# Two attention stages, convolutions and w_out rearranged: SSD and modulation beside the second attention, half of w_out beside the convolutions

## The chip, the cores and the metric

The kernel runs on one core of a Trainium2 chip. The metric is the device time of one execution in microseconds, inputs in DRAM at the start, output in DRAM at the end. Three runs of the kernel before gave 1917.51, 1924.35 and 1926.78 us; the median is 1924.35. Engines go by the names of the profile: PE (TensorE's matrix multiplies), PEld (its weight loads), DVE (VectorE), ACT (ScalarE), POOL (GpSimd) and SP (SyncE). POOL and SP do little but issue transfers here.

## The reference

Two layers act on 512 latent tokens and 256 context tokens of width 1024, in fp32. In each layer the normed tokens are projected and go through four head groups of width 256, whose outputs are concatenated and projected back; an MLP follows. The core of it:

```python
def token_mixers(h, hc, w_in, w_out, ...):
    proj, projc = h @ w_in, hc @ w_in
    ya, yac = ssd_branch(proj[..., :OFF_B], projc[..., :OFF_B], ...)
    yb = hyena_seq(proj[..., OFF_B:OFF_C], ...)
    yw = window_attention(apply_rope(qw, cos, sin), apply_rope(kw, cos, sin), vw, kwc, vwc, attn_sink)
    yd = dense_attention(apply_rope(rms_norm(qd, q_norm), cos, sin), ..., vd, kdc, vdc)
    y = jnp.concatenate([ya, yb, yw, yd], axis=-1) @ w_out
    if not need_ctx:
        return y, None
    ...
    return y, yc

def squared_relu_mlp(h, w1, w2):
    return jnp.square(jax.nn.relu(h @ w1)) @ w2
```

SSD is a chunked state space scan in two directions. Hyena multiplies spectra twice (two gated long convolutions), here done with matmuls against cosine and sine tables. The windowed attention ("c" in the kernel) and the dense one ("d") have 4 query heads and 2 key heads of 64. Around both halves of a layer stand norms with scale, shift and gate from a modulation vector, c @ w_mod. In the last layer the context outputs aren't needed.

## The kernel before

Every large product is made of three matmuls (`mm3`, lines 298 to 300): an operand is split into a rounded high part (`hi`, line 265 on ACT or 267 on DVE) and the difference (`lo`, line 270 on DVE), and high x high, high x low and low x high add up in PSUM. Tokens are in blocks of 128, six in layer 0 (four latent, two context) and four in layer 1. Weights arrive on SP's queue in units of 512 KB into raw tiles `r`, and are split into `w` with a priority of 4000 (`load_units`, 337).

The order of each engine comes from a scheduler that takes the instructions in program order, shifted by the priority they were written under; each engine then runs its list in order and waits where an instruction isn't ready. Where buffers of a pool come round, the next user waits for the last reader. `weave` (203) interleaves several generators, so many steps of each in turn.

After the setup and the hyena filters, `layer` (1379) does per layer:

- One stage with the pools `attR` and `ppA`: attention "d", the projection of "c", attention "c", then the projections of hyena and SSD. A block of attention goes from PE (`ps`, 1249 and 1250) to a maximum on DVE (1256), exp on ACT (1263), a scaling on DVE (1269), transposes on PE (1286), the split of the result into `pt` on ACT and DVE, and the product with V on PE (1294). The output is stored to the DRAM tensor `yy` (`y_d`) on POOL's queue (1299). The projections fill PE in between, since nothing of the attentions is needed by them.
- A stage with `ppB`, called mixing below: hyena for the latent tokens, hyena for the context (layer 0 only), SSD and the modulation vectors of the next sub-layers, woven. SSD reads its inputs back from DRAM (`xb`), hyena from `us`, its tables from `in_fwd` and `in_inv` (tiles `ht`, on POOL's queue) and its spectra `hf` on SP's queue.
- `ysplit`: the attention outputs are loaded from `yy` and split on DVE.
- `w_out` (1486) for pairs of token blocks: all four units of w_out, in the order 2, 3 (attention), 1, 0 (hyena, SSD), into PSUM `py`; `gated_norm` (1301) squares on ACT and scales on DVE (1311); `residual` and the pre-norm follow; then the MLP.

## Time and profile before

| | |
|---|---|
| median of three runs | 1924.35 us |
| the profiled execution | 1919.0 us, its span 1917.2 us |
| PE, DVE, ACT busy in the span | 1790.2, 1297.7, 836.8 us |
| layer 0: attentions and projections / mixing / w_out and norm | 151 to 405 / 405 to 543 / 543 to 620 us |
| layer 1: the same | 1210 to 1405 / 1405 to 1499 / 1499 to 1560 us |

The times of the stages are those between the first instructions of one stage's bound engine and the next. A busy share says how long an engine's instructions lay on it, not that they were fast: matmuls are pipelined, so what one matmul costs is the distance to the next one's start. The granted clock is the share of full speed that TensorE got in a stretch; full speed is 2.4 GHz, the other level is 1.2.

### The profile page before, as it was taken

Reading aid. Unit: us, or ns where it says so; the run is one execution under the profiler, and the core shown is the slowest. Engines: PE = TensorE matmul, PEld = TensorE weight load, DVE = VectorE, ACT = ScalarE, POOL = GpSimd, SP = SyncE. Lnnn points to the kernel's source line nnn. Section 1 sums busy time; section 2 is a strip of 40 time slices with the busy share of each in tenths; the row PEclk is TensorE's granted clock in tenths of the full one; section 3 lists DMA queues with packets and bytes.
Section 4 is the critical chain, followed back from the end, with each engine's and each line's share of the span. In section 5 each row is a group of like instructions: output and inputs, shape, how many; then the busy total and the mean of one; then the engine's idle time right before and its main releaser. Section 6 shows DMA issues by size and latency. Waiting matters only on the chain.

```text
span 1917.2 us, 27370 instructions
## 1 busy us (share of the span) xinstructions
PE 1790.2 (93%) x10170; PEld 1482.7 (77%) x10170; DVE 1297.7 (68%) x2897; ACT 836.8 (44%) x1804; POOL 91.5 (5%) x176
## 2 busy tenths in 40 slices
PE   6899999978879999999999998899978789999998
PEld 2688888845668888888888888888866688888886
DVE  4878888877756656676666658988878563444446
ACT  4844565536515532322222327556546263332322
POOL 0120001011000000000000000000010000000000
PEclk9999999989989999999999999999989899999999
DMA  8531121278833244333333415112183243233232
GB/s 291 187 111 53 39 74 58 69 260 272 290 107 132 93 135 136 121 107 114 121 121 121 142 47 176 45 48 89 45 273 120 74 157 113 91 99 99 88 102 85
DMA packets 137597, 235.16 MB, mean 123 GB/s; under 512 B 12466, under 2 KB 77395, under 8 KB 137464
## 3 DMA queue, kind: packets, MB, share of 16 engines
q1 hardware_dynamic: 122920, 186.12, 30.2%
q0 software_dynamic: 14544, 47.30, 7.1%
q8 instruction: 80, 1.31, 0.3%
q14 instruction: 53, 0.43, 0.1%
HBM read 206.74 MB, written 26.64 MB: 122 GB/s over the span
## 4 chain that ended last, share of the span: by engine, by line
PE 76%; DVE 9%; issue 6%; DMA 4%; ACT 4%; POOL 1%; SPq 0%; DVEq 0%; ACTq 0%; POOLq 0%
PE pg L298 19%; PE pg L299 18%; PE pg L300 18%; PE po L1294 3%; PE py L298 2%; PE py L299 2%; PE pm L1286 2%; PE py L300 2%; PE ps L1249 1%; PE ps L1250 1%; PE pm L1206 1%; PE psd L1052 1%; DMA spec<-fk 1%; POOL spec L725 1%; DMA r<-in_w_mod_dram 1%
## 5 line engine op out<-in xcount | busy, mean ns | idle before, releaser
L265 ACT ACTIVATE w<-r 128x1024 fp32r<-128x1024 f32 (+1 forms) x176 | 186.6, 1061 | 348.1 <-PE pg L300 325.1
L270 DVE TENSOR_TENSOR w<-r,w 128x1024 fp32r<-128x1024 f32 (+1 forms) x176 | 214.1, 1223 | 106.1 <-ACT w L265 105.2
L298 PE MATMUL pg<-xl,w 128*128 128x512 f32 (+1 forms) x704 | 269.5, 386 | 2.2 <-DVE ya L1311 0.9
L300 PE MATMUL pg<-xl,w 128*128 128x512 f32 (+1 forms) x704 | 269.7, 384 | 0.0
L299 PE MATMUL pg<-xl,w 128*128 128x512 f32 (+1 forms) x704 | 269.7, 384 | 0.0
L298 PE MATMUL pg<-w,H 128*128 128x512 f32 x640 | 250.1, 391 | 0.0
L299 PE MATMUL pg<-w,H 128*128 128x512 f32 x640 | 249.2, 390 | 0.0
L300 PE MATMUL pg<-w,H 128*128 128x512 f32 x640 | 249.0, 389 | 0.0
L476 DVE SCALAR_TENSOR_TENSOR x<-r,scT,x 128x512 f32<-128x512 f32 x168 | 119.1, 746 | 71.7 <-DMA r<-in_w_mod_dram 71.7
L298 PEld LDWEIGHTS pg<-xl,w 128*128 128x128 f32 x704 | 132.6, 190 | 27.7 <-issue 2.2
L300 PEld LDWEIGHTS pg<-xl,w 128*128 128x128 f32 x704 | 133.3, 189 | 22.9
L299 PEld LDWEIGHTS pg<-xl,w 128*128 128x128 f32 x704 | 133.3, 189 | 22.2 <-DVE xl L270 0.2
L298 PEld LDWEIGHTS pg<-w,H 128*128 128x128 f32 x640 | 120.1, 188 | 26.8 <-issue 1.7
L300 PEld LDWEIGHTS pg<-w,H 128*128 128x128 f32 x640 | 120.1, 188 | 25.0
L299 PEld LDWEIGHTS pg<-w,H 128*128 128x128 f32 x640 | 120.2, 188 | 24.4
L1520 ACT ACTIVATE t<-pg 128x512 f32<-128x512 f32 (+1 forms) x100 | 50.4, 506 | 198.0 <-PE pg L300 198.0
L1551 DVE TENSOR_TENSOR ya<-pg,ya 128x512 f32<-128x512 f32 x120 | 81.8, 687 | 69.0 <-PE pg L300 68.7
L1522 DVE TENSOR_TENSOR t<-t 128x512 f32<-128x512 f32 (+1 forms) x100 | 58.1, 582 | 83.7 <-ACT H L1521 83.6
L300 PE MATMUL pg<-xc,w 128*128 128x256 f32 (+1 forms) x368 | 104.4, 284 | 0.0
L298 PE MATMUL pg<-xc,w 128*128 128x256 f32 (+1 forms) x368 | 103.3, 284 | 1.1 <-ACT xc L265 1.1
L299 PE MATMUL pg<-xc,w 128*128 128x256 f32 (+1 forms) x368 | 104.1, 284 | 0.0
L298 PE MATMUL pg<-w,xl 128*128 128x256 f32 (+1 forms) x320 | 93.0, 292 | 5.4 <-ACT qk L1113 2.5
(357 smaller groups left out, 3866.1 us busy)
## 6 DMA issues: line engine op xcount, KB each, us to landing
r<-in_mlp_w_dram SPq DMA_DIRECT2D x128, 512.0 KB
r<-in_w_mod_dram SPq DMA_DIRECT2D x80, 512.0 KB
r<-in_w_in_dram SPq DMA_DIRECT2D x40, 512.0 KB
ht<-in_inv_dram POOLq DMA_DIRECT2D x20, 512.0 KB, 5.4
ht<-in_fwd_dram POOLq DMA_DIRECT2D x18, 512.0 KB, 5.4
wm<-in_w_mod_dram SPq DMA_DIRECT2D x16, 512.0 KB
r<-in_w_out_dram SPq DMA_DIRECT2D x16, 512.0 KB
xd<-x POOLq DMA_DIRECT2D x16, 512.0 KB, 3.3
```

The lines of the kernel that those rows point to most:

```text
L265: self.nc.scalar.activation(dst, src, AF.Copy)
L270: self.nc.vector.tensor_tensor(dst, src, h.bitcast(F32), SUB)
L298: mm(out, ah, bh, start=first, stop=False)
L299: mm(out, ah, bl, start=False, stop=False)
L300: mm(out, al, bh, start=False, stop=last)
L476: nc.vector.scalar_tensor_tensor(acc[:, c], raw[:, k], sc, acc[:, c], MUL, ADD)
L725: nc.gpsimd.dma_start(dst, kt[:, half, :])
L1286: nc.tensor.transpose(p[:, n:n + 128], P[:, col:col + 128], self.ident)
L1294: nc.tensor.matmul(po[:, qo:qo + m], V[:, c, :], pt[:, hl, cols[j]:cols[j] + m], start=i + j == 0 and hl == 0, stop=i + j == len(kts) - 1 ...
L1520: nc.scalar.activation(r, p[:, :nn], AF.Relu)
L1522: nc.vector.tensor_tensor(r, r, r, MUL)
L1551: nc.vector.tensor_tensor(dst, p, dst, ADD)
```

## The change

The projections of attention "c", SSD and hyena stand beside attention "d" alone, in that order (units z, x0, x1 before h0, h1, h2). Attention "c", SSD and modulation are woven in a stage of their own (`ppA2`), SSD in tiles that the projections and attention "d" used (`xl1`, `xc1`, `qk`, `V`). The attention's generator yields after each pair of blocks. `qk_split` transposes the raw q and k first and splits out of PSUM. Then come the convolutions, latent hyena with a priority of 4000 and context hyena with 1000, woven with `w_part`: the half of w_out that multiplies the attention outputs, per block of 128 tokens, evicted by ACT and stored on POOL's queue to a DRAM tensor `part`. `w_out` keeps units 1 and 0, and a DVE addition per block brings in `part`, which SP loads. `ysplit` is gone. Line numbers of the changed kernel differ: mm3 is at 299 to 301 there.

```diff
-        for br in "dc":
-            if br == "c":
-                self.qkv = self.qkv_in(l, br, XT)
-            qk, V = self.qkv
-            self.qk_prep(l, br, qk)
-            self.attention(l, br, qk, V)
+        self.do(self.attention(l, "d", *self.qkv))
+        self.qkv = self.qkv_in(l, "c", XT)
+        self.ssd_in(l, XT)
         self.hyena_in(l, XT)
-        self.ssd_in(l, XT)
+        self.pop(pp)
+
+        bk = {"ps": (1024, F32, 1), "po": (512, F32, 1), "pm": (512, F32, 3), "pd": (512, F32, 2)}
...
+        if mods:
+            bk.update({"pm": (512, F32, 2), "pmod": (512, F32, 1)})
+        pp = self.push("ppA2", bk, psum=True)
+        YT = self.new_xt((0,), need)
+        self.load_units(self.upos[l, "o", 3])
+        self.weave((self.attention(l, "c", *self.qkv), 1), (self.ssd(l, YT), 1), (chain(*mods), 3))
...
-        self.weave(*hys, (self.ssd(l, YT), W2[1]), (chain(*mods), W2[2]))
+        self.weave(*hys, (self.w_part(l, nt), 1))
...
+    def w_part(self, l, nt):
...
+        for t in range(nt):
+            y = self.t2((128, 4, 128))
+            nc.sync.dma_start(y, self.y_d[l][:, :, 128 * t:128 * t + 128].rearrange("c p t -> p c t"))
+            Y = [self.a("xl1", (4, 128)) for _ in range(2)]
+            self.hi(Y[0], y)
+            self.lo(Y[1], y, Y[0])
+            for q in range(2):
+                p = self.a("pw")
+                for c in (2, 3, 0, 1):
+                    w = self.utiles[l, "o", 2 + c // 2][q][:, :, c % 2]
+                    self.mm3(p, Y[0][:, c], Y[1][:, c], w[:, 0], w[:, 1], c == 2, c == 1)
+                o = self.t2()
+                nc.scalar.activation(o, p, AF.Copy)
+                nc.gpsimd.dma_start(self.part[l][t][:, 512 * q:512 * q + 512], o)
+                yield
...
-        order = (2, 3, 1, 0)
+        order = (1, 0)
...
+            nc.vector.tensor_tensor(ys[t], p, ys[t], ADD)
```

PE's list in layer 1, in the second attention. Before, between two blocks' `ps` rows and their transposes, stand rows of a projection (`pg`):

```order
L1249 MATMUL ps_13488<-QK_13262,QK_13260 128x256
L1250 MATMUL ps_13488<-QK_13263,QK_13260 128x256
L298 MATMUL pg_14205<-w_14119,xl_2105_11319 128x264
L299 MATMUL pg_14205<-w_14119,xl_2105_11319 128x264
L300 MATMUL pg_14205<-w_14119,xl_2121_11335 128x264
L298 MATMUL pg_14205<-w_14119,xl_2107_11321 128x264
L1286 MATMUL pm_13507<-ident,P_13481 128x128
L1286 MATMUL pm_13519<-ident,P_13481 128x128 x2
L1286 MATMUL pm_13530<-ident,P_13481 128x128
L299 MATMUL pg_14205<-w_14119,xl_2107_11321 128x264
```

The same place of the changed kernel (`pm` takes the attention's transposes, `po` its product with V):

```order
L1255 MATMUL ps_14062<-QK_13816,QK_13813 128x256
L1256 MATMUL ps_14062<-QK_13817,QK_13813 128x256
L1259 MATMUL ps_14062<-wmask,identr 128x256
L1255 MATMUL ps_14062<-QK_13816,QK_13813 128x256
L1256 MATMUL ps_14062<-QK_13817,QK_13813 128x256
L1292 MATMUL pm_14013<-ident,P_14006 128x128
L1292 MATMUL pm_14013<-ident,P_13987 128x128
L1292 MATMUL pm_14013<-ident,P_14006 128x128
L1292 MATMUL pm_14025<-ident,P_14006 128x128
L1292 MATMUL pm_14036<-ident,P_14006 128x128
L1300 MATMUL po_13891<-pt_14014,V_12717 128x256 x4
```

The projection rows have moved ahead of this place; here only the attention's own rows follow each other.

ACT's list in layer 1 at the start of the convolutions. `hx` are hyena's transformed inputs; ahead of them stood rows of SSD's convolution (`t`, line 735 and 914):

```order
L914 ACTIVATE t_14642<-t_14641 128x256
L734 ACTIVATE t_14680<-pg_14653 128x512
L735 ACTIVATE t_14678<-pg_14653,s_14409 128x512
L265 ACTIVATE hx_14739<-ph_2798_14734 128x512
L265 ACTIVATE hx_14773<-ph_2811_14768 128x512
```

In the changed kernel, where `xl_2801` is the high part of the first attention outputs, loaded back from `yy` into `t_14848`:

```order
L1305 ACTIVATE tA_14777<-po_14573 64x512
L266 ACTIVATE xl_2518_13757<-xl_2789_14808 128x512
L266 ACTIVATE xl_2519_13758<-xl_2791_14817 128x512
L266 ACTIVATE xl_2801_14850<-t_14848 128x512
L266 ACTIVATE hx_14845<-ph_2798_14840 128x512
L266 ACTIVATE hx_14875<-ph_2805_14870 128x512
```

The split of `w_part` stands ahead of both `hx` rows; before, nothing loaded from `yy` stood there. On DVE its low part stands ahead of the `hx` low parts too.

POOL's list in layer 1 at the same place. Before, the attention's last store stands three issues ahead of hyena's first tables, among stores of SSD's inputs:

```order
L1299 DMA yy_110<-yt_13684 128x512
L916 DMA xb_106<-t_14520 128x512
L916 DMA xb_106<-t_14557 128x256
L782 DMA ht_14793<-in_fwd_dram 128x1024
L916 DMA xb_106<-t_14604 128x512
L782 DMA ht_14833<-in_fwd_dram 128x1024
```

In the changed kernel:

```order
L1309 DMA yy_110<-yt_13890 128x512
L1309 DMA yy_110<-yt_14300 128x512
L784 DMA ht_14897<-in_fwd_dram 128x1024
L784 DMA ht_14945<-in_fwd_dram 128x1024
...
L1497 DMA part_0_117<-t_14867 128x512
L843 DMA ht_15316<-in_inv_dram 128x1024
L1497 DMA part_0_117<-t_14891 128x512
L843 DMA ht_15330<-in_inv_dram 128x1024
```

The tables now come directly after the last store of the attention, and the `part` stores come among and behind the later tables. On PE the last `pw` rows before `w_out`'s `py` in layer 1 read:

```order
L301 MATMUL pw_15126<-w_13685,xl_2852_15093 128x512
L299 MATMUL pw_15126<-w_13685,xl_2851_15092 128x512
L300 MATMUL pw_15126<-w_13685,xl_2851_15092 128x512
L301 MATMUL pw_15126<-w_13685,xl_2852_15093 128x512
L299 MATMUL py_15438<-wx_15417,xl_2520_13759 128x512
```

These rows stand behind the last hyena matmul; before, no such rows existed, and `py` followed on hyena.

## Rows read from the trace of the kernel before

**Rows 1.** Windows, layer 0: from:to, length, busy per engine, granted clock, DMA share, GB/s

```profile
151.00:405.00 254.00, 240.99 (x1618) 212.02 (x1617) 216.51 (x572) 144.15 (x372) 19.15 (x35) 0.98 0.22 69
190.00:300.00 110.00, 109.24 (x715) 94.86 (x716) 93.47 (x227) 67.34 (x168) 7.79 (x14) 1.00 0.18 55
405.00:543.00 138.00, 111.97 (x788) 74.72 (x788) 97.42 (x240) 67.99 (x207) 12.27 (x23) 0.87 0.78 261
426.00:543.00 117.00, 96.53 (x679) 66.69 (x679) 81.86 (x208) 61.80 (x192) 9.55 (x18) 0.88 0.75 253
400.00:426.00 26.00, 17.24 (x115) 9.13 (x115) 20.47 (x43) 7.39 (x17) 2.72 (x5) 0.75 0.94 312
543.00:620.00 77.00, 75.97 (x336) 62.01 (x337) 40.16 (x120) 31.43 (x55) 2.14 (x4) 0.96 0.40 141
```

**Rows 2.** Windows, layer 1

```profile
1210.00:1405.00 195.00, 185.89 (x1198) 158.95 (x1198) 166.69 (x413) 109.48 (x270) 10.44 (x19) 0.99 0.21 63
1405.00:1499.00 94.00, 65.48 (x394) 51.23 (x392) 73.75 (x166) 51.27 (x144) 9.61 (x18) 0.89 0.57 189
1405.00:1426.00 21.00, 9.93 (x45) 8.31 (x44) 12.62 (x21) 6.76 (x11) 4.84 (x9) 0.77 1.02 350
1470.00:1499.00 29.00, 17.27 (x122) 15.43 (x122) 25.60 (x62) 9.91 (x18) 1.06 (x2) 0.87 0.36 120
1499.00:1560.00 61.00, 56.80 (x256) 47.61 (x257) 33.87 (x87) 22.25 (x36) 2.14 (x4) 0.89 0.38 130
```

**Rows 3.** Chain of waits, layer 1, start of mixing: start us, us, what

```profile
1412.89 5.70 DMA xb<-t
1418.65 6.80 DMA sb<-xb
```

**Rows 4.** Chain of waits, layer 0, mixing

```profile
419.10 7.30 DMA ht<-in_inv_dram
...
485.86 5.57 DMA r<-in_w_mod_dram
...
496.70 5.29 DMA r<-in_w_mod_dram
```

**Rows 5.** Chain of waits, layer 1, w_out: an early and a later matmul

```profile
1501.17 0.43 PE py L299
...
1506.54 0.23 PE py L300
```

**Rows 6.** DVE groups, 151 to 405 us: line, shapes, count | busy, mean ns

```profile
L270 DVE TENSOR_TENSOR pt<-pm,pt 128x512 fp32r<-128x512 f32 x44 | 29.3, 688 | 8.8 <-ACT pt L265 8.4
...
L1256 DVE TENSOR_REDUCE s<-ps 128x1 f32<-128x768 f32 x16 | 15.3, 953 | 1.6 <-PE ps L1250 1.6
...
L270 DVE TENSOR_TENSOR sqk<-qk,sqk 128x128 fp32r<-128x128 f32 x48 | 12.2, 284 | 2.9 <-ACT sqk L265 2.9
...
L1209 DVE CAST QK<-pm 128x256 fp32r<-128x256 f32 x24 | 9.6, 419 | 0.6 <-ACT QK L1208 0.4
```

**Rows 7.** DMA issues: line, queue, count, KB each, median us to landing

```profile
us<-t POOLq DMA_DIRECT2D x12, 256.0 KB, 2.3
...
xb<-t POOLq DMA_DIRECT2D x8, 256.0 KB, 3.4
```

**Rows 8.** Chain of waits, layer 1, end of w_out, start of the MLP

```profile
1545.53 0.24 PE py L300
...
1552.48 0.58 PE pg L298
...
1559.13 0.48 PE pg L298 x4
```

**Rows 9.** Line L1311, the norm's last step: duration ns min/median/max

```profile
L1311 DVE SCALAR_TENSOR_TENSOR ya<-py,s,gt x10: 1273/1280/1284, 573.3 to 1551.2; 128x1024 f32<-128x1024 f32 x10
```

More of the change, by code (lines that the diff above doesn't have):

```diff
@@ L2 @@
 import math
-from contextlib import ExitStack
+from contextlib import ExitStack, nullcontext
 import numpy as np
@@ L203, in weave @@
     def weave(self, *gens):
-        live = [[g, n, self.st, self.lab] for g, n in gens]
+        live = [[g[0], g[1], self.st, self.lab, g[2] if len(g) > 2 else 0] for g in gens]
         while live:
@@ L209, in weave @@
                 self.mark(e[3])
-                for _ in range(e[1]):
-                    if next(e[0], self) is self:
-                        live.remove(e)
-                        break
+                with self.tc.high_priority(offset=e[4]) if e[4] else nullcontext():
+                    for _ in range(e[1]):
+                        if next(e[0], self) is self:
+                            live.remove(e)
+                            break
                 e[2], e[3] = self.st, self.lab
@@ L424, in setup @@
         self.y_d = [self.tc.dram_tile([4, 128, NTOK], F32, name=f"yy{l}") for l in range(self.nl)]
+        self.part = [[self.tc.dram_tile([128, D], F32, name=f"part{l}_{t}") for t in range(NT)] for l in range(self.nl)]
         self.spec = {(l, n): self.tc.dram_tile([n // 128, 128, 1024], F32, name=f"spec{l}_{n}")
@@ L1025, in ssd @@
                 tk = slice(128 * t, 128 * t + 128)
-                p = self.a("ps")
-                nc.tensor.matmul(p[:, 0:256].rearrange("p (g i) -> p g i", g=2), bt[:, tk], ct[:, :, tk], start=True, stop=True)
-                sc = self.a("sf", (2, 2, 128))
+                ct = self.a("xc1", (2, 128), F32)
+                for gi in range(2):
+                    r_, z_ = slice(64 * gi, 64 * gi + 64), slice(64 - 64 * gi, 128 - 64 * gi)
+                    nc.vector.memset(ct[z_, gi], 0.0)
+                    nc.sync.dma_start(ct[r_, gi], self.xb_d[l][3, r_, tk])
+                p = self.a("pm")
+                nc.tensor.matmul(p[:, 0:256].rearrange("p (g i) -> p g i", g=2), bt[:, tk], ct, start=True, stop=True)
+                sc = self.a("xl1", (2, 2, 128), F32)
                 for d in range(2):
@@ L1062, in ssd @@
                         c0 = 256 * d + 128 * gi
-                        nc.tensor.matmul(po[:, c0:c0 + 128], ct[:, gi, tk], before[d, t], start=True, stop=True)
-                yo = self.a("sf", (2, 256))
+                        nc.tensor.matmul(po[:, c0:c0 + 128], ct[:, gi], before[d, t], start=True, stop=True)
+                yo = self.a("xl1", (2, 256), F32)
                 ds = slice(4 * dirs[0], 4 * dirs[-1] + 4)
@@ L1210, in qk_split, with turned @@
-        return QS, KS
+        QS = [[self.a("QK") for _ in range(2)] for _ in range(2)]
+        KS = [[self.a("QK") for _ in range(2)] for _ in range(2)]
+        lo, hi = slice(0, 64), slice(64, 128)
+        for t0, cnt in ((0, 4), (4, 2)):
+            n = 128 * cnt
+            cs = slice(128 * t0, 128 * t0 + n)
+            src = [qk[t // 2][:, t % 2] for t in range(t0, t0 + cnt)]
+            def turned(c0):
+                p = self.a("pm")
+                for i in range(cnt):
+                    nc.tensor.transpose(p[:, 128 * i:128 * i + 128], src[i][:, c0:c0 + 128], self.ident)
+                return p
+            p = turned(256)
+            for kv in range(2):
+                r = slice(64 * kv, 64 * kv + 64)
+                H, L = KS[kv]
+                for d in (lo, hi):
+                    nc.scalar.activation(H[d, cs], p[r, :n], AF.Copy)
+                for d in (lo, hi):
+                    nc.vector.tensor_tensor(L[d, cs], p[r, :n], H[r, cs].bitcast(F32), SUB)
+            if t0 == 0 or need:
+                for kv in range(2):
+                    p = turned(128 * kv)
+                    for hh in range(2):
+                        r = slice(64 * hh, 64 * hh + 64)
+                        Q = QS[kv][hh]
+                        nc.scalar.activation(Q[lo, cs], p[r, :n], AF.Copy)
+                        nc.vector.tensor_tensor(Q[hi, cs], p[r, :n], Q[lo, cs].bitcast(F32), SUB)
+            yield
@@ L1212, in attention @@
+        return list(zip(QS, KS))
     def attention(self, l, br, qk, V):
-        ops = [self.qk_split(l, kv, qk) for kv in range(2)]
+        self.qk_prep(l, br, qk)
+        yield
+        ops = yield from self.qk_split(l, qk)
         for kv, (QS, KS) in enumerate(ops):
-            self.attend(l, br, kv, QS, KS, V[kv], False)
+            yield from self.attend(l, br, kv, QS, KS, V[kv], False)
             if l < DEPTH - 1:
-                self.attend(l, br, kv, QS, KS, V[kv], True)
+                yield from self.attend(l, br, kv, QS, KS, V[kv], True)
@@ L1470, in layer @@
         pp = self.push("ppM", {"pg": (512, F32, 6)}, psum=True)
[L1471 removed]
+        r = self.mlp(l, XT2, (XTp,), nt, more, todo[0])
         self.pop(hp)
@@ L1479, in layer @@
         return r[0], r[1], fa
+    def w_part(self, l, nt):
+        self.mark("w_part")
+        nc = self.nc
+        self.st = "o"
+        for t in range(nt):
+            y = self.t2((128, 4, 128))
[11 more added lines that the diff above has]
+                nc.gpsimd.dma_start(self.part[l][t][:, 512 * q:512 * q + 512], o)
+                yield
     def w_out(self, l, YT, ys, t0):
         self.mark("w_out")
-        order = (2, 3, 1, 0)
+        order = (1, 0)
         if t0 == 0:
```

128 lines of the change are left out of this document (38 added, 90 removed).

## The prediction, made before the result was known

> **What bounds the kernel now.** I read the windows first, because the change touches two stretches of each layer and leaves the filters ahead and both MLPs alone. While both attentions run beside the projections, PE is the bound: in 110 us of the first layer it is busy for 109, at full clock, and DVE for 93 [rows 1]. The mixing stage that follows (SSD, both hyenas and, in layer 0, modulation) is another matter: of 138 us PE is busy 112 and DVE 97, at a mean granted clock of 0.87 [rows 1]; in layer 1, of 94 us PE is busy 65 and DVE 74 [rows 2]. No engine is full there; chains wait for each other and for transfers. Its first 21 us in layer 1 hold 10 us of PE and 13 of DVE, while DMA is full [rows 2]. The chain of waits shows why: a tile goes out to DRAM in 5.70 us and comes back in 6.80 [rows 3], and in layer 0 a filter table (7.30 us) and raw modulation weights (5.57 and 5.29) are waited for on the path [rows 4]. Only w_out runs on PE alone again: 76 us busy of 77 in layer 0, 57 of 61 in layer 1 [rows 1, 2], the first matmuls at 0.43 us, the later ones at 0.23 [rows 5].
>
> So what can be won is some 26 us of idle PE in layer 0's mixing stage and 29 in layer 1's, and the change tries it in two ways: SSD and modulation go beside the second attention, and half of w_out's matmuls under the convolutions. What can be lost is that the second attention no longer has projections to keep PE full.
>
> **The change part by part.** Work on an engine is counted from the new order, each instruction at the mean of its row, scaled so that the same count of the kernel before gives its busy time; the large rows of DVE are [rows 6]. In the whole program PE and DVE hardly change: DVE goes from 1298 to about 1301 us. What counts is where it stands. I use two efficiencies from rows: DVE's busy share is 85% (93.47 of 110) beside projections [rows 1], 88% (25.60 of 29) where hyena is nearly alone, and 70% (81.86 of 117) in layer 0's mixing after its first stall [rows 1, 2].
>
> *First attention.* The transposes of q and k now come ahead of the split: 64 instead of 176 transposes, and 56 larger DVE instructions in place of 88 differences of 284 ns (48 of them in layer 0) and 44 copies of 419 [rows 6], 32 us in place of 35: some 3 us off DVE in all. The stage has 105 us of DVE and 103 of PE to the attention's end in layer 0, so it lasts 105/0.86 = 122 us. Then 389 projection matmuls are left with no attention beside them: 192 with 512 columns at 0.23 and 197 with 256 at about half, 67 us, taken as 68. Layer 1: 89/0.87 = 102, then 212 and 48 matmuls, 54, taken as 57 for the convolution rows behind them.
>
> *Second attention with SSD (and modulation).* In layer 0 DVE has 233 instructions of attention (72 us), 98 of SSD (38) and 8 of modulation (3), about 10 us of it done before the projections end: 103 left, and PE has 81, ACT 99. PE's order shows no pg rows between the softmax pieces any more (first pair of lists in the section on the change), so DVE is the bound and PE is idle about 40%. The efficiency isn't in the trace of before, which has no such mixture; the bounds are 70% and 92%, giving 147 and 112 us. I take 83%, nearer to the 88 of hyena alone than to the 70, since the stall of the store and load round trip now lies beside the attention's work: 124, and 7 for the first and last steps and a modulation weight waited for: 131. Layer 1: 81 less 6 in advance, 75/0.84 = 89, plus 6: 95 (82 to 107).
>
> *Convolutions with half of w_out.* The second attention's last yy store stands on POOL's queue ahead of hyena's tables, and the first y load waits for it: store and load again, 12.5 us [rows 3]. In layer 1 ACT's split of that load stands ahead of both hx rows (second list), so hyena waits for all of it; in layer 0 it stands behind the first, so I count 5. Then hyena: in layer 0 DVE has 61 us in the stage, of which about 48 fall before the last latent hyena matmul, 48/0.88 = 54, and after that PE's order has 23 us of w_part and 6 of context hyena still to come: 5 + 54 + 29 = 88 (78 to 100). Layer 1: 12.5 + 41.9/0.88 = 60, and 10 us of PE behind: 70 less 1 for overlap, 69 (58 to 78). So the work to be hidden, 33 us in layer 0 and 22 in layer 1, is hidden by about 10 and 12; the rest is only moved. The removed first stall (21 us with 10 of PE [rows 2], 26 with 17 in layer 0 [rows 1]) is what pays for it.
>
> *Stores and loads added.* 20 part stores, 10 loads of y and 10 of part, 256 to 512 KB. The nearest rows are the 256 KB stores on POOL, 2.3 and 3.4 us to landing [rows 7]; a store and load on the path is 12.5. The part loads stand on SP's queue ahead of MLP weights, but the first is needed only when w_out's second half starts: I take 0, with 5 us each layer for the range, and nothing below 0, since nothing is removed from that queue but eight y loads. The Trainium skill prices this otherwise: "DMA: Bandwidth & Descriptors", section on the SWDGE path, fits 2.0 us plus bytes over 436e3 per us. By it a 256 KB store and load is an estimated 5.2 us; by it the convolution stage of layer 1 would be 7 us shorter. The trace doesn't agree at this place (12.5), and the row is used.
>
> *w_out's second half and norm.* 96 instead of 192 matmuls in layer 1: 96 x 0.23 = 22 us; from PE's last py matmul (1545.53) to the first of the MLP (1552.48) lie 7 us, and the MLP runs dense only at about 1560 [rows 8]: 15. The new add on DVE takes about as long as L1311, 1.28 us [rows 9], twice per pair: 2.6. With 3 for a slow clock at the start: 42, against 61. Layer 0: 144 x 0.23 = 33, plus 15, the add, and 1.4: 52, against 77. The 16 y splits on DVE that are gone (10 us) ran before this part, and are inside the stage figures.
>
> *The sum.* Layer 0: before 254 + 138 + 77 = 469; after 122 + 68 + 131 + 88 + 52 = 461, so -8. Layer 1: before 195 + 94 + 61 = 350; after 102 + 57 + 95 + 69 + 42 = 365, so +15. Net +7 on a profiled execution of 1919.0 us, 1926; the median of the runs is 5.35 above that execution, so 1931.
>
> **The rivals.** *Faster: the second attention and SSD feed DVE well.* Two independent chains could keep DVE at 92%: 112 and 82 instead of 124 and 89, so -19 in all, and if ACT's split waits less than 12.5 and the tail of w_part slips under context hyena, -15 more: 1897. For it: DVE reaches 85% even where PE is full. Against it: 70% is what SSD, hyena and modulation made together.
>
> *Slower: PE and DVE wait for each other.* The place is the second attention. A softmax block goes PE, DVE, ACT, DVE, PE, ACT, DVE, PE; before, the projections filled PE in between, now only SSD's rows do, as serial, and ps has one buffer as before. At 70% the stage is 147 instead of 124 in layer 0, and at 75% 100 instead of 89 in layer 1; with two modulation weights waited for on PE's order at about 5.4 us [rows 4], 45 us: 1976 at its full size, about 1958 at half. It decides from about 82% of DVE in both stages: below that the sum is over +0.5%.
>
> *Clock.* In mixing the granted clock was 0.87 and 0.89, in the attention stages 0.98 and 0.99 [rows 1, 2], and w_out's first matmuls took 0.43 us after the slack before it [rows 5]. With PE 62% busy in the new stage I expect the levels seen where it was 60% busy, 0.87 (17.27 of 29 us [rows 2]); PE's 81 us grow to 93, still under DVE's. If it stayed at the lower level throughout, 81 became 162 us and 53 became 106: +31 and +11, 1973. The Trainium skill, "TensorE: Matmul & The Clock Gate", section on HAM oscillation, says that waits between groups of matmuls throttle the engine again and again; it speaks against a stage with sparse matmuls, and the 0.87 row agrees in sign, not to the full price.
>
> *The change doesn't do what it says.* It would be so if all of w_part came behind hyena; the order shows 10 of 33 us ahead of that point, so it is a matter of degree, in the range above.
>
> **How the numbers follow.** A difference of 0.5%, 9.6 us, is about what can be told from no change. Forecast: within that, 1931 (chance 0.36). Faster, around 1897: 0.30. Slower, 0.34: of it 0.29 for engines waiting for each other and 0.05 for the clock. The stage bounds (112 to 147, 78 to 100, 82 to 107, 58 to 78, 10 for loads) don't all fall to one side; the range reaches from the faster rival, 7 us beyond its figure, to the half-sized slower one and 12 beyond: 1890 to 1970. The forecast's own range is 1915 to 1934.
>
> **What would show it.** In the profile after: DVE's busy share in the second attention (right if 80 to 86%, the sum wrong if over 90 or under 75); PE dense for about 65 and 54 us after each first attention; hyena's first matmuls some 12 us after the last yy store in layer 1; PE busy only with pw rows for 20 us at the end of layer 0's convolutions; and stretches of 52 and 42 us from the first py matmul to the MLP. Most likely to be wrong is the second attention's length, 131 and 95: one tenth in efficiency moves the total by about 24 us.

## The result and the profile after

The changed kernel takes 2041.05 us (median of four runs, 2035.46 to 2044.55) against 1923.83 of the kernel before in the same runs: a ratio of 1.061, with a 95% interval from 1.057 to 1.065. It is 117 us slower where 7 were forecast, outside the range of 1890 to 1970.

The windows of the changed kernel, with the borders moved to its own stages (from:to, length, busy per engine in the order PE, PEld, DVE, ACT, POOL, then granted clock, DMA share, GB/s). Layer 0:

```profile
151.00:355.00 204.00, 193.82 (x1295) 173.44 (x1294) 147.39 (x325) 97.72 (x214) 15.72 (x29) 1.00 0.24 72
355.00:533.00 178.00, 133.81 (x799) 83.22 (x797) 117.18 (x342) 101.46 (x307) 4.10 (x8) 0.84 0.37 120
533.00:641.00 108.00, 81.87 (x436) 67.80 (x436) 58.20 (x119) 24.45 (x44) 17.83 (x34) 0.89 0.64 203
641.00:697.00 56.00, 41.49 (x173) 32.62 (x174) 41.76 (x111) 29.50 (x48) 2.69 (x5) 0.82 0.65 228
```

and layer 1, which now begins at 1290 instead of 1210:

```profile
1290.00:1451.00 161.00, 150.87 (x936) 132.52 (x935) 122.72 (x275) 77.04 (x154) 9.72 (x18) 0.97 0.28 86
1451.00:1573.00 122.00, 85.12 (x417) 60.83 (x415) 85.77 (x226) 69.06 (x205) 3.39 (x7) 0.80 0.08 24
1573.00:1647.00 74.00, 55.71 (x305) 47.29 (x304) 48.98 (x86) 22.75 (x36) 10.53 (x20) 0.85 0.74 243
1647.00:1678.00 31.00, 25.35 (x109) 20.45 (x110) 20.70 (x53) 12.70 (x21) 1.61 (x3) 0.93 0.61 206
```

The four rows of a layer are the first attention with all projections, the second attention with SSD, the convolutions with w_part, and the rest of w_out up to the MLP's first matmul. (The forecast's last term ran a little further, to the dense MLP: 3 us in layer 0, 7 in layer 1; the table adds them.)

| us | before | forecast | measured | miss |
|---|---|---|---|---|
| layer 0: first attention, projections | 254 with both attentions | 190 | 204 | +14 |
| second attention, SSD, modulation | in 138 of mixing | 131 | 178 | +47 |
| convolutions, w_part | in the same 138 | 88 | 108 | +20 |
| w_out to MLP | 77 | 52 | 59 | +7 |
| layer 1: first attention, projections | 195 with both attentions | 159 | 161 | +2 |
| second attention, SSD | in 94 of mixing | 95 | 122 | +27 |
| convolutions, w_part | in the same 94 | 69 | 74 | +5 |
| w_out to MLP | 61 | 42 | 38 | -4 |

The second attention's stage holds 74 of the 118 us missed. Against [rows 1, 2]: DVE's share there is 66% and 70%, lower than 85% beside projections, and no engine is over 76% busy. What the engines wait for in layer 1, between the first and the last exp of that attention, reads, largest first (engine, its instruction <- the one it waited for: us in total, times, longest), first for ACT, then DVE, then PE:

```profile
ACT P L1269 <- DVE s L1265: 17.3, 6, 3.8
ACT pt L266 <- PE pm L1292: 7.7, 4, 2.3
...
DVE xl L1048 <- ACT xl L1046: 8.8, 6, 2.7
DVE s L1273 <- ACT s L1272: 5.3, 6, 1.2
DVE s L1262 <- PE ps L1256: 4.1, 5, 1.8
...
PE ps L1255 <- ACT P L1269: 9.4, 8, 2.6
PE pd L1044 <- ACT xl L1042: 4.7, 3, 2.0
```

Each engine waits for the others, and in the whole view there is no DMA among the releasers: ACT's exp for DVE's maximum, DVE for PE's scores and ACT's exp, PE for ACT's exp before it may overwrite the scores. Rows of SSD (`pd`, `xl`) stand among them in the same lists.

The pace of an attention says the same more briefly. The exp of a block (line 1263 before, 1269 after) gives one record per block of 128 queries; for the 24 blocks of layer 0's second attention the line's own view reads, before and after (duration min/median/max, first and last start):

```profile
L1263 ACT ACTIVATE P<-ps,s x24: 468/690/801, 292.1 to 389.5; 128x512 f32<-128x512 f32 x8, 128x640 f32<-128x640 f32 x8, 128x256 f32<-128x256 f32 x8
```

```profile
L1269 ACT ACTIVATE P<-ps,s x24: 464/687/797, 388.7 to 523.5; 128x512 f32<-128x512 f32 x8, 128x640 f32<-128x640 f32 x8, 128x256 f32<-128x256 f32 x8
```

From first to last that is 4.24 us a block before (97.4 over 23) and 5.86 after; in layer 1 4.63 and 5.57. The first attention, which kept its projections, goes at 3.89 (4.18 before) and 4.54 (4.47). And the first exp comes 34 us after the last projection in layer 0 (354.6 to 388.7) and 26 in layer 1 (1450.7 to 1476.6).

### The profile page after: what moved, and what is told of

Its sections match the earlier page's. It is cut to its first block, busy times and chain, and to the rows that moved or that the text cites. A ratio compares the mean times of both kernels' runs of the same rounds, so it can differ in the third digit from the quotient of the medians.

```text
span 2042.3 us, 27173 instructions
## 1 busy us (share of the span) xinstructions
PE 1831.3 (90%) x10058; PEld 1499.1 (73%) x10058; DVE 1313.3 (64%) x2833; ACT 852.5 (42%) x1758; POOL 101.9 (5%) x196
## 4 chain that ended last, share of the span: by engine, by line
PE 62%; issue 18%; DVE 9%; DMA 6%; ACT 5%; POOL 1%; SPq 0%; DVEq 0%; ACTq 0%; POOLq 0%
PE pg L299 17%; PE pg L300 17%; PE pg L301 17%; PE po L1300 2%; DVE t L743 1%; DMA r<-in_w_mod_dram 1%; PE ps L1255 1%; DMA spec<-fk 1%; PE pw L301 1%; DVE w L271 1%; DMA ht<-in_inv_dram 1%; DMA gt<-gated 1%; DMA t<-yy 1%; PE pw L299 1%; PE pw L300 1%
```

## Experiments

Below, "pace" is the exp-to-exp distance per block, worked out as above.

### The second attention written ahead of SSD

```diff
-        self.weave((self.attention(l, "c", *self.qkv), 1), (self.ssd(l, YT), 1), (chain(*mods), 3))
+        self.do(self.attention(l, "c", *self.qkv))
+        self.weave((self.ssd(l, YT), 1), (chain(*mods), 3))
```

> The changed kernel, but the second attention is written in full ahead of SSD and modulation, so that it has priority and SSD only fills its gaps. The changed kernel's second attention with SSD took 177 us in layer 0 and 118 in layer 1, where 131 and 95 were forecast. Theory A (the two chains, written in turn, get in each other's way on the in-order lists): the stage becomes shorter, under 105 us in layer 1 and 155 in layer 0, total 2000 us or less. Theory B (each chain by itself is a row of short steps on three engines and the stage is as long as these steps, whatever the order): layer 1 within 10 us of 118, total within 25 us of 2041.

Measured: 2063.11 us (before 1925.59), one run. Windows: layer 0 attention, then what is left of SSD, and the same in layer 1:

```profile
350.00:488.00 138.00, 103.55 (x633) 61.84 (x632) 88.84 (x254) 65.01 (x186) 3.79 (x7) 0.79 0.44 147
488.00:550.00 62.00, 39.39 (x176) 26.25 (x176) 34.35 (x97) 36.67 (x122) 3.73 (x7) 0.75 0.26 84
1460.00:1560.00 100.00, 68.36 (x293) 51.03 (x292) 67.84 (x173) 45.07 (x121) 1.08 (x2) 0.69 0.07 22
1560.00:1601.00 41.00, 30.02 (x127) 21.45 (x126) 22.20 (x58) 25.33 (x85) 3.73 (x7) 0.71 0.36 116
```

Theory A falls: the stage became longer, 200 and 141 us. Theory B's figure for the stage of layer 1 (within 10 us of 118) is missed as well; its total holds (22 us over 2041). But the attention's pace is back to 4.26 and 4.43 us, what it was before the change, without projections and with PE now 75% busy at a clock of 0.79 in layer 0 and 68% at 0.69 in layer 1. Here an attention goes at the same pace beside a PE that is partly idle as it did beside a full one. The timeline of one block shows the ring (start us, us, engine, line):

```profile
1509.62 0.80 ACT L1269 ACTIVATE P<-ps,s 128x640 f32<-128x640 f32 x1 [1.90 <-DVE s L1265]
...
1510.56 0.45 PE L1255 MATMUL ps<-QK,QK 128*128 128x384 f32 x1 [2.62 <-ACT P L1269]
...
1511.63 0.82 DVE L1262 TENSOR_REDUCE s<-ps 128x1 f32<-128x640 f32 x1
...
1512.47 1.30 ACT L266 ACTIVATE pt<-pm 128x512 fp32r<-128x512 f32 x2 [1.78 <-PE pm L1292]
...
1512.74 0.15 DVE L1265 TENSOR_SCALAR s<-s 128x1 f32<-128x1 f32 x1
...
1513.66 0.79 ACT L1269 ACTIVATE P<-ps,s 128x640 f32<-128x640 f32 x1
```

The exp ends, PE may write the next scores into the one `ps` buffer (1510.56), DVE takes their maximum (1511.63), the scaled maximum is ready at 1512.89, ACT is still at the split of the last block (1512.47), then comes the next exp: 4.04 us around. The last 0.77 us of them are a wait for ACT's own order, not for the buffer.

### Modulation beside the convolutions

```diff
-        self.weave((self.attention(l, "c", *self.qkv), 1), (self.ssd(l, YT), 1), (chain(*mods), 3))
+        self.weave((self.attention(l, "c", *self.qkv), 1), (self.ssd(l, YT), 1), (chain(), 3))
...
-        self.weave(*hys, (self.w_part(l, nt), 1))
+        self.weave(*hys, (self.w_part(l, nt), 1), (chain(*mods), 2))
```

> The changed kernel, but the modulation vectors of layer 0 are woven with the convolutions instead of the second attention; layer 1 is unchanged. Theory C (the wait of PE's list for the raw modulation weights is what lengthens layer 0's second attention): that stage falls from 177 to 140 us or less. Theory B (attention and SSD set it by themselves): it falls by no more than 20 us, and the convolutions, which share DMA with 16 MB of weights now, grow by 10 to 30, total 2030 to 2060.

Measured: 2090.77 us, one run. Layer 0's stage fell only to 166 us and the next grew to 165:

```profile
352.00:518.00 166.00, 114.19 (x529) 84.51 (x528) 115.64 (x335) 95.63 (x292) 3.58 (x7) 0.76 0.09 28
518.00:683.00 165.00, 110.71 (x715) 75.23 (x713) 62.99 (x131) 30.57 (x60) 18.91 (x36) 0.82 0.69 228
```

Theory C falls: without any modulation, and with a DMA share of 0.09, the second attention still goes at 5.60 us a block. The convolutions grew by 57 us, twice what I expected at most, and the total lies above the 2030 to 2060 of Theory B.

### Two score buffers beside SSD

```diff
+        if not need:
+            bk.update({"ps": (1024, F32, 2), "pm": (512, F32, 2), "pd": (512, F32, 1)})
```

> The changed kernel, but in layer 1 the scores of the second attention have two PSUM buffers (ps) and in exchange the transposes two (pm) and SSD one (pd). Theory D (the one ps buffer, whose next block waits for the exp of the last, is what sets the stage): layer 1's second attention falls from 118 to 100 us or less, total 2020 or less. Theory B: it stays within 10 us of 118 or grows, as SSD has one buffer less.

Measured: 2046.13 us, one run; pace in layer 1 5.90, the stage 129 us. That is no gain, but SSD and the transposes each lost a buffer in exchange, so the run doesn't show what a second score buffer alone would do beside SSD.

### PE kept busy with matmuls nobody needs

```diff
+            for _ in range(25):
+                p = self.a("pf")
+                for i in range(10):
+                    nc.tensor.matmul(p[:, 0:384], self.identr, self.wmask, start=i == 0, stop=i == 9)
```

> The changed kernel, but in layer 1's second attention 250 matmuls of 384 columns on constants, whose results nobody reads, fill PE's gaps at the lowest priority, and the transposes have two PSUM buffers instead of three. Theory E (TensorE's lower clock, 0.59 to 0.84 in the first half of that stage, is what lengthens it): with PE kept busy the granted clock is near 1.00 and the stage falls from 118 to 105 us or less although about 42 us of matmuls are added. Theory B (short steps on several engines): the clock rises, the stage stays at 115 to 135 us.

Measured: 2045.19 us, one run. The second attention's stage of layer 1:

```profile
1449.00:1572.00 123.00, 113.49 (x666) 92.06 (x665) 85.29 (x226) 69.07 (x205) 2.67 (x5) 0.97 0.07 24
```

The granted clock rose from 0.80 to 0.97, PE carried 250 matmuls more, and the stage is 123 us instead of 122, the pace 5.54 instead of 5.57. The faster clock and the filled PE together changed nothing. The run alone doesn't exclude that a gain from the one and a cost of the other cancel; the run with the attention written first, where a block took 4.26 us at a clock of 0.79 as it had at full clock, speaks against it. Room for 250 matmuls of 384 columns lay free beside this attention, and the change had taken the projections out of it. Theory E falls, and Theory B's range holds.

### Two score buffers in the kernel before

```diff
-PM = (3, 2, 1)
+PM = (2, 1, 2)
```

(buffers of `pm`, `pg` and `ps`)

> The kernel before with two PSUM buffers for the scores of an attention instead of one, in exchange two instead of three for its transposes and one instead of two for the projections. Attention blocks follow each other there at 4.2 to 4.6 us (exp to exp), with PE full or idle. If the ring exp, next scores, maximum, exp over one buffer sets that pace, it falls to 3.5 us or less, and the stage is then as long as PE's work: 10 to 30 us less in both layers together. If it is DVE's and ACT's in-order lists, it stays over 4, and with one buffer for projections the total is over 1925.

Measured: 1999.38 us, ratio 1.041 (1.037 to 1.044). The exps of layer 0's first attention:

```profile
L1263 ACT ACTIVATE P<-ps,s x24: 457/899/905, 185.6 to 255.5; 128x768 f32<-128x768 f32 x16, 128x256 f32<-128x256 f32 x8
```

3.04 us a block instead of 4.18 (3.83, 3.18 and 4.31 for the other three, which took 4.24, 4.47 and 4.63). But three buffer counts changed at once, and with one buffer the projections fell behind. Their matmuls (tile `pg`) between the first and the last exp of that attention, in this run and in the kernel before (from:to, length, busy of PE, PEld, DVE, ACT on `pg`, clock, DMA share, GB/s):

```profile
185.60:255.50 69.90, 23.14 (x144) 19.30 (x144) 2.34 (x11) 3.84 (x18) 1.00 0.12 34
```

```profile
183.70:279.80 96.10, 60.86 (x319) 46.05 (x319) 2.58 (x12) 11.25 (x32) 1.00 0.16 50
```

That is 2.1 projection matmuls a us instead of 3.3. So the gain can't be put down to the score buffer alone. Against the thinner projections as the whole reason stands that the second attention, written first and without any projections, was no faster with one buffer (4.26 and 4.43), though some rows of SSD stood beside it there. The ring over the one score buffer is likely to be a limit, but this run doesn't isolate it. When the attentions were done, 86 us of projections were left:

```profile
151.00:363.00 212.00, 189.31 (x1238) 162.93 (x1238) 172.23 (x487) 120.12 (x323) 9.18 (x17) 0.97 0.14 42
363.00:449.00 86.00, 63.26 (x380) 54.55 (x379) 39.28 (x79) 23.88 (x46) 9.18 (x17) 0.96 0.29 95
```

### The same, with the projections' second buffer kept

```diff
-PM = (3, 2, 1)
-SF = (5, 6, 8, 8)
+PM = (1, 2, 2)
+SF = (5, 6, 6, 8)
```

> The kernel before with two PSUM buffers for the scores, two for the projections as they had, and one instead of three for the attention's transposes (and SSD's six scratch tiles in layer 1). With two score buffers and one for projections, blocks came at 3.0 to 4.3 us, but the projections lasted 50 to 65 us longer than the attentions. If the ring over the one score buffer sets the pace and the projections only needed their second buffer, the stage is as long as PE's work, 235 to 250 us in layer 0 instead of 254: total 1890 to 1915, a version better than both. If the one transpose buffer takes the ring's place, blocks come at 4.5 us or slower and the total is 1925 to 1960.

Measured: 1944.83 us, ratio 1.010 (1.006 to 1.013). Blocks come at 4.07 to 4.75 us, hardly another pace than with one score buffer, and the projections keep theirs. Whether the one buffer for the transposes took the ring's place, or the score buffer never was what counted, the run doesn't tell apart. Neither of the two other ways of dividing PSUM that I tried is faster than the first.

### The second attention beside the projections again

```diff
         self.qkv = self.qkv_in(l, "c", XT)
+        self.do(self.attention(l, "c", *self.qkv))
...
-        self.weave((self.attention(l, "c", *self.qkv), 1), (self.ssd(l, YT), 1), (chain(*mods), 3))
+        self.weave((self.ssd(l, YT), 1), (chain(*mods), 3))
```

> The changed kernel with one thing undone: the second attention stands with the projections again, beside which it stood in the kernel before; SSD and modulation have the stage after it for themselves; convolutions and w_part stay as changed. Theory B (an attention lasts about as long whether PE is full or not, so projections beside the first alone leave 54 to 67 us of them uncovered, and SSD beside the second lengthens it): attentions and projections take 245 to 265 us in layer 0 and 185 to 200 in layer 1, as before the change, SSD alone 60 to 75 and 40 to 50, total 1935 to 1975. Rival F (the slower part is the convolutions with w_part and what stands behind, not the attention): the total stays over 2010.

Measured: 1996.3 us, ratio 1.039 (1.036 to 1.041): 45 us of the loss are undone, less than expected. Attentions and projections, then SSD with modulation, then the convolutions of layer 0; below them SSD and the convolutions of layer 1:

```profile
151.00:397.00 246.00, 230.90 (x1540) 203.45 (x1539) 211.00 (x525) 140.32 (x328) 17.09 (x32) 0.99 0.20 62
397.00:511.00 114.00, 77.68 (x510) 39.05 (x508) 51.16 (x144) 55.85 (x184) 5.59 (x11) 0.78 0.65 217
511.00:615.00 104.00, 81.09 (x432) 68.02 (x432) 56.05 (x110) 24.42 (x44) 14.49 (x27) 0.89 0.54 172
...
1469.00:1531.00 62.00, 42.48 (x172) 26.50 (x172) 30.15 (x86) 33.71 (x116) 3.74 (x7) 0.64 0.26 83
1531.00:1597.00 66.00, 56.41 (x308) 47.03 (x308) 47.37 (x82) 21.98 (x35) 9.13 (x17) 0.89 0.67 214
```

The first row is right (246, expected 245 to 265): two attentions cover all projections of layer 0 as before. In layer 1 they don't quite: the second attention goes at 5.47 us a block beside the projections, nearly as slowly as beside SSD (5.57), and ends 19 us behind them (1469 against 1450):

```profile
L1269 ACT ACTIVATE P<-ps,s x16: 670/742/798, 1378.9 to 1461.0; 128x512 f32<-128x512 f32 x8, 128x640 f32<-128x640 f32 x8
```

From the first exp to that end are 180 us, where the kernel before took 162 (1233.6 to 1396.0). What I had too low above all is SSD by itself: 114 and 62 us, with DVE at 45 to 49% of them and PE at 68%. No full engine sets its length either. In the kernel before it lay beside hyena: both together took 138 and 94 us [rows 1, 2]; apart they take 114 + 104 and 62 + 66, the second figures with `w_part`.

### The split of q and k of the second attention beside the projections

```diff
         self.qkv = self.qkv_in(l, "c", XT)
+        self.qk_prep(l, "c", self.qkv[0])
+        g = self.qk_split(l, self.qkv[0])
+        while True:
+            try:
+                next(g)
+            except StopIteration as e:
+                ops = e.value
+                break
...
-        self.weave((self.attention(l, "c", *self.qkv), 1), (self.ssd(l, YT), 1), (chain(*mods), 3))
+        self.weave((self.attention(l, "c", *self.qkv, ops), 1), (self.ssd(l, YT), 1), (chain(*mods), 3))
```

> The changed kernel, but the rotary step and the split of q and k of the second attention stand in the first stage, ahead of SSD's and hyena's projections, so that they run beside those. In the changed kernel 34 us in layer 0 and 26 in layer 1 lie between the last projection and the first exp of the second attention (388.7 and 1476.6 us), of which the prediction counted 7 and 6. Theory G (this start is laid bare by the change, since the projections that covered it before are used up): it falls to under 10 us in each layer, the total by 35 to 50 us, to 1990 to 2005. If the blocks then become slower by as much (above 6.5 us a block, SSD being met by more of them), the total stays over 2025.

Measured: 2025.87 us, ratio 1.054 (1.051 to 1.058): 15 us gained, less than half of what I expected. The start did shrink, from 34 to 5 us and from 26 to 6, and the attention ended at 498 and 1529 instead of 531 and 1568. But SSD, which ended last in the changed kernel already (534 and 1573), still ended at 531 and 1562: its stretch went from 179 and 122 us to 173 and 115. A gain on one chain of a stage counts only until the other is last. And the pace of layer 1's attention:

```profile
L1270 ACT ACTIVATE P<-ps,s x16: 677/739/800, 1452.6 to 1521.7; 128x512 f32<-128x512 f32 x8, 128x640 f32<-128x640 f32 x8
```

Beside the same SSD it is 4.60 us a block, as without SSD (in layer 0 it is 5.69). So whose rows stand beside an attention doesn't alone set its pace.

### Half of the second attention beside each

```diff
+        self.do(att2(0))
         self.ssd_in(l, XT)
...
-        self.weave((self.attention(l, "c", *self.qkv, ops), 1), (self.ssd(l, YT), 1), (chain(*mods), 3))
+        self.weave((att2(1), 1), (self.ssd(l, YT), 1), (chain(*mods), 3))
```

(`att2(kv)` is the attention of one key head; the early split is kept)

> The changed kernel with the early split of q and k, and one of the two key heads of the second attention beside the projections again, the other beside SSD: between the run with the early split (2026) and the one with the whole second attention beside the projections (1996). Theory B/G (projections left without an attention are the price, 72 and 58 us, and an attention beside SSD takes 5.6 us a block): blocks beside SSD are half as many, SSD (113 and 62 us alone, 173 and 115 with a whole attention) is met by half the rows, total 1980 to 2005. If SSD is as long with half an attention as with a whole one, the total is over 2015.

Measured: 1995.45 us, ratio 1.038 (1.034 to 1.042), as expected. SSD with half an attention takes 137 and 87 us, between the 114 and 62 alone and the 173 and 115 with a whole one (the early split's run):

```profile
383.00:520.00 137.00, 105.21 (x645) 57.98 (x644) 77.75 (x232) 73.92 (x237) 6.46 (x12) 0.84 0.57 183
1451.00:1538.00 87.00, 62.78 (x285) 45.57 (x284) 53.38 (x145) 49.24 (x156) 4.29 (x8) 0.76 0.23 75
```

So each block of an attention that SSD meets lengthens it by 2 to 3.3 us (59 us over 24 blocks, 23 over 12, 53 over 16, 25 over 8), against the 4.2 to 4.6 that a block of it took beside the projections in the kernel before.

### One part alone: the new split of q and k in the kernel before

```diff
-        ops = [self.qk_split(l, kv, qk) for kv in range(2)]
+        ops = self.qk_split(l, qk)
```

(with the changed `qk_split`, without its yields)

> The kernel before with one part of the change alone: q and k are transposed first and split out of PSUM. By the prediction's step it takes some 3 us of DVE off each program and 112 transposes off PE, beside a full PE: 1918 to 1924, between 0 and 0.3% faster. Theory B, in which the attention's chain sets the stage, gives the same sign but up to 8 us, as the split stands at the start of each attention's chain, four times.

Measured: 1946.44 us, ratio 1.014 (1.010 to 1.018): slower by 25 us, against a forecast of a small gain. The projections are done at 387 us in layer 0, and the attention goes on alone for 23 us; in layer 1 26:

```profile
151.00:387.00 236.00, 228.37 (x1535) 203.02 (x1534) 200.74 (x487) 134.29 (x313) 16.38 (x30) 0.99 0.20 61
387.00:410.00 23.00, 14.47 (x56) 10.67 (x58) 16.16 (x50) 10.13 (x28) 1.62 (x3) 0.58 0.22 75
...
1414.00:1440.00 26.00, 16.85 (x77) 13.06 (x76) 18.01 (x44) 11.69 (x28) 1.08 (x2) 0.71 0.44 137
```

Before, projections and attentions ended within 3 us of each other in layer 0 (396.5 and 394.0). The part has less work and yet loses: in layer 0 the projections end 9 us earlier, and blocks go at 4.6 to 5.1 us in three of four attentions. That the order which comes with it does this is likely, but why the scheduler's list shifts so far I didn't test. In the changed kernel itself, where other rows stand beside it, the first attention doesn't show it (3.89 and 4.54).

### One part alone: half of w_out beside the mixing of layer 1

```diff
+        wp = not need
...
-        self.weave(*hys, (self.ssd(l, YT), W2[1]), (chain(*mods), W2[2]))
+        self.weave(*hys, (self.ssd(l, YT), W2[1]), (chain(*mods), W2[2]), *([(self.w_part(l, nt), 1)] if wp else []))
...
-        order = (2, 3, 1, 0)
+        order = (1, 0) if self.wp else (2, 3, 1, 0)
...
-SF = (5, 6, 8, 8)
+SF = (5, 6, 6, 8)
```

> The kernel before with one part of the change alone, in layer 1: the attention half of w_out is multiplied beside the convolutions and SSD (where PE is idle 29 of 94 us) and added behind; the splits of the attention outputs go. SSD has six scratch tiles instead of eight, to make room. If the idle PE takes the 22 us of matmuls, w_out falls from 61 to about 46 and mixing grows by no more than 8: 1910 to 1918. Rival F (w_part's transfers and splits lengthen the convolutions by as much as w_out gains): 1920 to 1932.

Measured: 1925.63 us, ratio 1.0016 (1.0002 to 1.0030). w_out to the MLP fell from 53 to 38 us and mixing grew from 93 to 113 (both to the first matmul):

```profile
1406.00:1519.00 113.00, 88.77 (x483) 70.12 (x481) 74.56 (x165) 56.65 (x155) 14.10 (x26) 0.89 0.58 190
1519.00:1557.00 38.00, 27.81 (x110) 21.91 (x109) 29.66 (x63) 16.02 (x23) 1.07 (x2) 0.81 0.52 165
```

PE had 29 us idle there, and using 23 of them cost 20, as Rival F had it. Two runs look for the reason. The first is the kernel before with only the smaller scratch of that run:

```diff
-SF = (5, 6, 8, 8)
+SF = (5, 6, 6, 8)
```

> The kernel before, but SSD has six scratch tiles instead of eight in layer 1, as in the run that put half of w_out beside layer 1's mixing, where mixing ended 19 us later than before. If the scratch tiles did that, mixing of layer 1 is longer by 10 us or more here too (total 1930 to 1940); if w_part's rows did it, it is longer by at most 4 (total 1918 to 1928).

Measured: 1918.01 us, ratio 0.998 (0.997 to 1.000); mixing is 3 us shorter, if anything. The smaller scratch is not what lengthened it. The second gives hyena and SSD a priority over w_part:

```diff
-        hys = [(self.hyena(l, SEQ, 0, YT), W2[0])]
+        hys = [(self.hyena(l, SEQ, 0, YT), W2[0], 0 if need else 1000)]
...
-(self.ssd(l, YT), W2[1]),
+(self.ssd(l, YT), W2[1], 0 if need else 1000),
```

> The kernel before with half of w_out beside layer 1's convolutions and SSD, as in the earlier run, but hyena and SSD have a priority of 1000 over it. If w_part's rows, standing among those of hyena on the in-order lists, lengthened mixing by 19 us, it is now longer by 8 to 14 (what is left over comes behind hyena on PE alone), total 1912 to 1922. If it is the transfers or the tiles, mixing stays 19 longer, total 1922 to 1930.

Measured: 1926.93 us, ratio 1.003 (1.001 to 1.005). Hyena ends at 1491.9, earlier than in the run without priority (1515.2), but w_part is last now, at 1529.9 instead of 1471, and SSD ends at 1520, later than without the priority (1502). Mixing is 27 us longer than in the kernel before (from the last projection to w_out), more than either forecast; w_out to the MLP falls to 35. The total lies where I had put transfers or tiles; the tiles are excluded, and that hyena moves with its priority shows that the order of the rows matters. Why SSD became later, and whether w_part's transfers hold the rest, stays open.

### The same in both layers

```diff
-        self.weave(*hys, (self.ssd(l, YT), W2[1]), (chain(*mods), W2[2]))
+        self.weave(*hys, (self.ssd(l, YT), W2[1]), (chain(self.w_part(l, nt), *mods), W2[2]))
```

> As the last, in both layers; in layer 0 the half of w_out shares one PSUM buffer with modulation and comes ahead of it, SSD has four scratch tiles instead of five, hyena five instead of six. If idle PE takes it: w_out of layer 0 falls from 77 to 57, mixing grows by 5 to 12 as modulation starts later, total 1895 to 1912. Rival F: modulation, begun later, ends the stage later by 20 or more, total 1920 to 1945.

Measured: 1945.35 us, ratio 1.013 (1.010 to 1.016). Layer 0's modulation starts at 499 instead of 408 us and ends at 586 instead of 517; mixing ends 46 us later. That is Rival F's sign in layer 0; the smaller buffers of SSD and hyena there were not tried alone.

No version came out ahead of the kernel before by more than the 0.2% of the scratch tiles.

## Why the prediction was wrong

**The reading of the bound** was half right. PE was full beside the projections [rows 1], and I took that to mean that the attention leans on PE. The runs show that it doesn't: a block took 4.24 us in layer 0 with PE full, and 4.26 and 4.43 without any projections and with PE 75% and 68% busy. A full PE and a slow chain were there at once. Projections were therefore nearly free beside *either* attention, and taking them from the second laid them bare behind the first: 72 us in layer 0 and 58 in layer 1. That part of the sum I had (68 and 57). What I didn't see is that nothing pays for it. What does set a block's pace is shown only in part. In the timeline the ring over the one score buffer takes 3.3 of the 4.04 us, but the run that doubled the buffer also thinned the projections, and the one that kept them gained hardly anything. Nor is there one pace: layer 1's second attention goes at 5.47 us beside projections in one run and at 4.60 beside SSD in another. The order of the rows on the in-order lists counts as well as their number; what decides it stays open.

**The second attention** is the step that failed. I divided DVE's work by an efficiency of 83%, between bounds of 70 and 92, and got 131 and 95 us. DVE was busy for 66% and 70%, at and below the lower bound. These shares lie under the 75% that the prediction had named as the sign of a wrong sum. The work was mis-sized too: 117 and 86 us of DVE lay in the stage where I had counted 103 and 75, since hardly any of it ran ahead of the projections' end. But even that work at 83 and 84% would be 141 and 102 us, not 178 and 122. Dividing by a busy share was itself the mistake: the stage holds two chains of short steps on three engines that wait for each other, and with no engine over 76% busy its length comes from these waits. The attention takes 138 us in layer 0 and 100 in layer 1 with its start, where it is written first, and SSD alone 114 (with modulation) and 62. Put side by side they take 178 and 122, less than the sum but more than either. The start that I counted at 6 to 7 us took 26 to 34, but it is not the cause by itself: with it gone, SSD was still last and only 15 us came back. The rival "PE and DVE wait for each other" had the right place and mechanism; its full price, 45 us, stood in the text, and the range took half of it. (Half of 45 on 1931 is 1953.5, not 1958, so the range should have ended near 1966.) Measured are 74 over the forecast.

**The convolutions.** The 12.5 us for a store and a load on the path in layer 1 were right: the chain of waits reads, start us, us, what,

```profile
1570.30 2.93 DMA yy<-yt
1573.24 10.21 DMA t<-yy
1583.48 0.64 ACT xl L266
```

13.1 us to the split, with hyena's `hx` rows behind it. Layer 1 came to 74 (forecast 69). In layer 0 it was 108 against 88. Up to the end of the latent hyena's matmuls and behind it (columns as in the result):

```profile
533.00:601.00 68.00, 50.40 (x292) 44.19 (x293) 40.34 (x83) 13.99 (x26) 13.51 (x26) 0.82 0.81 251
601.00:641.00 40.00, 31.47 (x146) 23.61 (x144) 17.86 (x37) 10.46 (x19) 4.33 (x8) 1.00 0.36 122
```

So 9 us were lost ahead of that point (forecast 5 + 54) and 11 behind it (forecast 29). Ahead of it the chain waits for hyena's tables again and again:

```profile
533.91 7.47 DMA ht<-in_fwd_dram
...
553.43 6.32 DMA ht<-in_inv_dram
...
579.46 4.57 DMA ht<-in_fwd_dram
...
586.13 4.43 DMA ht<-in_inv_dram
```

I had priced only the y load on that queue. That the tables stand behind the attention's last store explains little: with the second attention beside the projections the first six tables are issued at 424 to 427, 84 us ahead of the stage, and it still takes 104. The later tables wait until PE is done with an earlier one (POOL waited 16.2 and 19.8 us for `ph` ahead of those issues) and then take 4 to 8 us each; how much of the 20 us that makes stays open.

**The other estimate of the store and load**, 5.2 us by the Trainium skill, "DMA: Bandwidth & Descriptors", section on the SWDGE path, is far from 13.1; the row decided rightly. Of that, 2.93 us are the store, near the Trainium skill's fit of 2.6; the load on SP's queue, 10.21 us with six table loads issued around it, is what that fit for a single transfer on POOL's path doesn't cover. In layer 0 the same kind of load took 3.02 us, with a DMA share of 0.52 there against 1.09:

```profile
629.73 3.02 DMA t<-yy
```

**The first attention**, +14 in layer 0: it ended after 131 us instead of 122, and 72 us of projections followed instead of 68. The first exp came 5 us later (189.3 against 183.8), but not by the change: in the four runs that leave this stage as it is, the first exp lies between 184.5 and 190.4. **w_out** was near: 59 and 38 against 52 and 42. **The new split**, costed at 3 us gained, costs 25 when put alone into the kernel before; how much of the 117 it makes in the changed kernel stays open, since there the first attention's pace doesn't show it. **The clock** as a rival is not borne out: at 0.97 instead of 0.80, with 250 matmuls more, the stage was as long, and an attention's blocks took 4.26 us at 0.79 as at full clock.

## What to carry to other kernels

Before moving work between stages, measure each chain's own pace (the distance from one record of a step to the next) with and without company: a stage whose chains of short steps set its length need not get shorter when an engine is freed, and an engine's busy share can't be turned into a duration. Work that fills gaps for nothing, here the projections, should lie beside every such chain, not beside one of them; moving it away pays only if the chain it leaves becomes shorter. And two chains on the same in-order lists lengthen each other here (in layer 1 122 us together, where the attention written first takes 100 and SSD alone 62), and a gain on one counts only until the other is last.

## What the runs showed of the hardware that I had not expected

Adding 250 matmuls of 384 columns to a stage of 122 us raised TensorE's granted clock from 0.80 to 0.97 and left the length at 123. An attention block took 4.24 us at full clock and full PE, and 4.26 at a clock of 0.79. And a 256 KB load took 10.21 us at a DMA share of 1.09, among six table loads, and 3.02 at a share of 0.52.
